# The MLP on unnormalised h: each token's squared norm factor moves behind w_down, and h is turned quarter by quarter

## The chip, the cores and the metric

The kernel runs on one core of one Trainium2 chip. The metric is the device time in microseconds (us) of one execution. The profile is one further execution, recorded by the hardware profiler.

## What is computed

A decoder block on 512 tokens of 1024 channels: two token mixers (a gated delta rule and a forgetting attention), merged by sigmoid gates, and behind them an MLP. All of it is float32. The change touches the last four lines alone:

```python
def rmsnorm(x, g):
    y = xf * lax.rsqrt(jnp.mean(xf * xf, axis=-1, keepdims=True) + EPS)
    return y * g
...
h = x + merged @ w_out[l]
hn = rmsnorm(h, norm_mlp_g[l])
x = h + jnp.square(jax.nn.relu(hn @ w_up[l])) @ w_down[l]
```

With r the factor rsqrt(mean(h²) + EPS) of a token, `hn` is r · (h · g). Since r is positive, relu(r · a)² = r² · relu(a)², so r² can be applied to a token's row behind `w_down`.

## The kernel before

**Arithmetic on TensorE.** Each float32 operand is split into a high and a low part (`hi` and `lo` of a weight, `shi` and `slo` of an activation), and a product is three matmuls: high by high, low by high, high by low. ScalarE (ACT) casts the high part (line 1165 for weights, 973 for activations), VectorE (DVE) subtracts to get the low part (1172 and 978).

**Seven products for eight.** From `w_o` (w_out) on, each big matrix product is done in the Strassen-Winograd way: a weight matrix is cut into quarters, and seven products P1 to P7 of sums of quarters stand for eight. Each of them is taken in two parts, s = 0 and s = 1. Weight sums are made by transfers: a plain load issued by SP, or one issued by POOL (GpSimd) that adds a further quarter to a tile in place, and can thus not start before the DVE has taken the low part of that tile's last contents. A part of a product needs one 128x1024 weight tile; its `hi` lies in one of four buffers, cast three parts ahead.

**Tokens and quarters.** The residual stream lies in `accs[tb][l]`: tb = 0 to 3 blocks of 128 tokens, l = 0, 1 halves of 512 channels. i = tb // 2 names a half of the tokens, and (i, l) a quarter of h. `w_o` and `w_d` (w_down) have the tokens on the partitions (`tokens_product`: 12 matmuls of 128x512 a part); after the second part of a product, its two PSUM tiles are added to one or two quarters of `accs` (`add_product`, `add_task`, DVE). `w_u` (w_up) has the features on the partitions (`blocks_product`: 24 matmuls of 128x256 a part) and reads h transposed: the tiles `hq[l][i, j]`. Those are made in `turn_h`: transposes on TensorE into PSUM tiles `hnT`, and ACT's copy to `hq` with the factor norm_mlp_g per partition (line 1112).

**PSUM.** All eight banks go in pairs: U for P1, then also for P6, P7 and P4, V for P5, then also for P3, W for P2, X for P4 of `w_o`. P3's first matmul goes on accumulating in V, so it waits for the additions that read P5 there; P7's waits likewise for P6's.

**Order.** `MLP` is the written list of parts: for `w_o` P1, P2, P1, P2 (parts 0, 0, 1, 1), then P5, P3, P6, P7, P4, two parts each; then `w_u` P1, P2, P5 and so on, `w_u` and `w_d` interleaved over four chunks of the hidden layer. The loop over it emits, for each part: what lies in `before` (the turns), the cast of the weight three ahead, the additions (`evicted`) of the part before, the low part, loads, up to three tasks out of `later`, and the matmuls. TensorE's order is kept as written (`PIN`); for DVE, ACT and POOL a scheduler sets the order at build time, and each engine then runs its queue in that order.

**The norm in the middle.** `h_done(i, l)` comes when a quarter of h has had its last addition: ACT squares and sums its rows (1085). When both quarters of a token half are done, `rms_h` makes r (DVE 1092 and 1093, then `rsq`, a power on POOL at line 306), `scale_h` writes r · h into pages `proj` (DVE, 1100, four of them), and `turn_h` turns the two quarters, 16 transposes of `proj` in one go.

Of the kernel before, what the change touches and what calls it, by code (L numbers as in the profile page):

```python
# [11 lines left out]
ALU = mybir.AluOpType  # L12
# [4 lines left out]
P = 128  # L17
T = 512
D = 1024
KT = D // P  # L20
H = 8
NCH = T // P
EPS = 1e-6
# [18 lines left out]
def hybrid_block(tc, a, out):  # L42
# [20 lines left out]
    def nm(s):  # L63
        n_names[0] += 1
        return f"{s}_{n_names[0]}"
# [5 lines left out]
    def page(dt=F32, s="pg"):  # L71
        if s in FOX_TAGS:
            return fxp.tile([P, T], dt, tag=s, name=nm(s))
        tag = TAGS_OF.get(s, s)
        if tag in TAGS:
            return pgp.tile([P, T], dt, tag=tag, name=nm(s), bufs=TAGS[tag])
        return pgp.tile([P, T], dt, tag="pg", name=nm(s))

    KEEP = ("ones", "expo", "ident", "c_norm_mlp_g", "rs_h", "ss_h")

    def const(shape, s, dt=F32):
        return (cp if s in KEEP else cm).tile(shape, dt, tag=s, name=s)

# [6 lines left out]
    def atps(s="at"):  # L90
        return pat.tile([P, T], F32, tag="at", name=nm(s))
# [7 lines left out]
    def cs(c):  # L99
        return slice(c * P, (c + 1) * P)  # L100
# [126 lines left out]
    def dense(nme, rhi, rlo, cols=P):  # L227
        hi, lo = unit(nme)
        ps = mmps()
        o = ps[:cols, :]  # L230
        for k in range(KT):
            w = hi[:, k * cols:(k + 1) * cols]
            mm(o, w, rhi(k), start=(k == 0), stop=False)  # L233
            mm(o, w, rlo(k), start=False, stop=False)  # L234
        tick()
        for k in range(KT):
            mm(o, lo[:, k * cols:(k + 1) * cols], rhi(k), start=False, stop=(k == KT - 1))  # L237
        return ps
# [14 lines left out]
    ones = const([P, P], "ones")  # L253
# [3 lines left out]
    expo = const([P, 16], "expo")  # L257
    vec.memset(expo, -0.5)
    ident = const([P, P], "ident")
# [45 lines left out]
    def rsq(dst, src):  # L305
        pool.tensor_tensor(dst, src, expo[:, 0:src.shape[-1]], op=ALU.pow)
# [40 lines left out]
    for pool_, tag, n in early:  # L347
        t = pool_.tile([P, n * T], F32R, tag=tag, name=nm("xs"))
# [12 lines left out]
    for k in range(KT):  # L361
        w = first[0][0][:, k * 64:(k + 1) * 64]
# [517 lines left out]
    def lst(ts_, j):  # L880
        return lambda k: ts_[k][j]
# [22 lines left out]
    for h in range(H):  # L904
        ps = dense("w_ga", uh, ul)
# [11 lines left out]
    for n in range(KT):  # L917
        ps = dense("w_pg", lst(oa, 0), lst(oa, 1))
# [10 lines left out]
    def accpage(s):  # L929
        return accp.tile([P, T], F32, tag="acc", name=nm(s))  # L930
# [5 lines left out]
    def of_half(pg_, f):  # L936
        return pg_[:, f * 256:(f + 1) * 256]
# [11 lines left out]
    pvec, pact, ppe = [Pinned(eng, pin) for eng, pin in zip((vec, act, nc.tensor), pins)]  # L949
    later = []  # L950
# [30 lines left out]
    def forms_later(qs, res, steps, parts=range(NSUB), front=False):  # L981
        new = [(form_task, qs[s_], res, p, s_, st) for p, st in steps for s_ in parts]
        later[:] = new + later if front else later + new
# [14 lines left out]
    for n in range(KT):  # L998
        ps = dense("w_gb", uh, ul)
# [4 lines left out]
    for n in range(KT):  # L1004
        s_, j, f = n // 4, n // 2 % 2, n % 2
        ps = dense("w_pf", lst(obs, 0), lst(obs, 1))
# [17 lines left out]
    accs = [[accpage("acc") for _ in range(2)] for _ in range(NCH)]  # L1024
# [6 lines left out]
    def apart(w, c):  # L1031

        return w == "w_o" or (w, c) == ("w_d", NC - 1)

    def banks(w, c, p, s_):
        b, first = ("X", True) if apart(w, c) and p == "P4" else BANKS[p]
        if first and s_ == 0:
            banks_of[w, c, b] = [atps("mlp"), atps("mlp")]
        return banks_of[w, c, b], first
# [11 lines left out]
                ppe.matmul(ps[t], slo[:, k], wh, start=False, stop=False, skip_group_check=True)  # L1051
                ppe.matmul(ps[t], shi[:, k], wl, start=False, stop=last, skip_group_check=True)

    def add_task(acc, ps, op):
        pvec.tensor_tensor(acc, acc, ps, op=op)  # L1055

    def count(w, c, i, l, done):
        n = left[w, c, i, l] = left.get((w, c, i, l), 0) + 1
# [3 lines left out]
    def add_product(w, c, p, ps, done):  # L1062

        add, sub = ALU.add, ALU.subtract
        for i, l, op in {"P1": [(0, 0, add)], "P2": [(0, 0, add)], "P5": [(1, 1, add)], "P3": [(0, 1, add)],
                         "P6": [(0, 1, sub)], "P7": [(1, 1, sub)] + ([(1, 0, add)] if apart(w, c) else []),
                         "P4": [(1, 0, add)]}[p]:
            for t in range(2):
                yield add_task, accs[2 * i + t][l], ps[t], op
            yield count, w, c, i, l, done  # L1070


    hq = quarters("hq")
    hforms = {}
    rs_h = const([P, NCH], "rs_h")
    ss_h = const([P, NCH, 2], "ss_h")

    before = []

    ready = [2, 2]  # L1080

    def h_done(i, l):
        for t in range(2):
            junk = page(s="junk")
            pact.activation(junk, accs[2 * i + t][l], AF.Square, accum_out=ss_h[:, 2 * i + t, l:l + 1])
        ready[i] -= 1
        if not ready[i]:
            later[:0] = [(rms_h, i), (scale_h, i, 0), (scale_h, i, 1)]

    def rms_h(i):  # L1090
        sl = slice(2 * i, 2 * i + 2)
        pvec.tensor_tensor(rs_h[:, sl], ss_h[:, sl, 0], ss_h[:, sl, 1], op=ALU.add)
        pvec.tensor_scalar(rs_h[:, sl], rs_h[:, sl], 1.0 / D, EPS, op0=ALU.mult, op1=ALU.add)
        rsq(rs_h[:, sl], rs_h[:, sl])

    def scale_h(i, l):
        hn = []
        for t in range(2):
            x = page(s="proj")
            pvec.tensor_scalar(x, accs[2 * i + t][l], rs_h[:, 2 * i + t:2 * i + t + 1], None, op0=ALU.mult)  # L1100
            hn.append(x)
        before.append((turn_h, i, l, hn))

    def turn_h(i, l, hn):
        for j in range(2):
            pt = atps("hnT")
            for f in range(2):
                for t in range(2):
                    ppe.transpose(pt[:, f * 256 + t * P:f * 256 + (t + 1) * P], hn[t][:, cs(2 * j + f)], ident)
            for f in range(2):  # L1110
                n = 4 * l + 2 * j + f
                pact.activation(of_half(hq[l][i, j], f), of_half(pt, f), AF.Copy, scale=mlp_g[:, n:n + 1])
        if l:
            forms_later(hq, hforms, SUMS if i else (("P1", "a"), ("P1", "b"), ("P2", "a"), ("P2", "b")), front=True)

    mlp = {}

# [35 lines left out]
    for k, (w, c, p, s_) in enumerate(MLP):  # L1153
# [26 lines left out]
        ps, first = banks(w, c, p, s_)  # L1180
        if w == "w_u":
            if p == "P1" and s_ == 0:
                mlp[c] = quarters("act"), {}
            qs, forms = mlp[c]
            blocks_product(c, p, s_, [hforms[k] for k in needs], ps, first)
            evicted = [(evict, p, qs[s_], ps[s_])]
            if s_ == NSUB - 1 and p in MADE:
                steps = MADE[p]
                if p == "P4" and c == NC - 1:
                    steps = sorted(steps, key=lambda st: ("P5", "P6", "P3", "P7", "P4").index(st[0]))  # L1190
                evicted.append((forms_later, qs, forms, steps))
        else:
            tokens_product(c, p, s_, res[p, s_], ps, first)
            done = h_done if w == "w_o" else give if c == NC - 1 else lambda i, l: None
            evicted = list(add_product(w, c, p, ps, done)) if s_ == NSUB - 1 else []
# [81 lines left out]
```

## Time and profile before

| | before |
|---|---|
| median of 3 runs | 1024.31 us (1021.71 to 1024.59) |
| profiled execution, and its span | 1024.1 us, 1022.4 us |
| mean granted clock of TensorE | 0.993 |
| TensorE busy | 1003.3 us, 98% of the span |
| DVE, ACT, POOL busy | 674.4, 561.5, 219.8 us |

The span runs from the first to the last instruction on the profile's own clock, and 1.7 us of the profiled execution lie around it. `w_o` begins at 651.7 us in the span, the first part of `w_u` at 694.3 us, and from there to the end TensorE has only products of the MLP. In lists of the trace a row gives the start and the length of an instruction (matmuls overlap, so their starts tell the pace), its line, its output and inputs, and in brackets how long its engine had idled before it and what ended that. The row of a timeline can hold several instructions (x16), whose length is then that of all. In a list of windows a row gives the length of the window, each engine's busy time in it and the granted clock (1.00 is full).

### The profile page before, as it was taken

How to read it: one execution, taken by the hardware profiler on the slowest of the kernel's cores; microseconds unless marked ns; L12 is line 12 of the kernel's file. 1: busy time of each engine (PE TensorE's matmuls, PEld its weight loads, DVE VectorE, ACT ScalarE, POOL GpSimd, SP SyncE). 2: the span in 40 equal slices, each digit the busy share in tenths (PEclk: the TensorE clock that was granted, in tenths of full speed). 3: DMA queues.
4: the chain of work that ended last, by engine and by line, in shares of the span. 5: the costliest groups of instructions: out<-in, count | busy, mean ns of one | idle time of the engine just before them, and what ended most of it. 6: DMA issues, size and time to landing. Idle time of an engine off the chain costs nothing.

```text
span 1022.4 us, 16241 instructions
## 1 busy us (share of the span) xinstructions
PE 1003.3 (98%) x6361; PEld 887.9 (87%) x6361; DVE 674.4 (66%) x1138; ACT 561.5 (55%) x855; POOL 219.8 (21%) x212
## 2 busy tenths in 40 slices
PE   8999999999999999999999999998999999999997
PEld 6788899998788999988888888778989989988985
DVE  6877677454657686354655225778897697687694
ACT  6765454546664455346753332557865665666751
POOL 1445130113532310113100004411121121121110
PEclk9999999999999999999999999999999999999999
DMA  6435322134433233123435534576888888788845
GB/s 214 144 110 150 96 81 84 56 108 128 124 101 114 58 111 95 53 93 114 126 113 172 196 103 157 120 180 123 195 177 206 181 175 216 171 176 197 191 89 127
DMA packets 58732, 138.67 MB, mean 136 GB/s; under 512 B 6208, under 2 KB 22816, under 8 KB 58656
## 3 DMA queue, kind: packets, MB, share of 16 engines
q1 hardware_dynamic: 48256, 99.88, 30.4%
q0 software_dynamic: 10400, 37.76, 20.8%
q8 instruction: 50, 0.82, 0.3%
q14 instruction: 26, 0.21, 0.1%
HBM read 129.18 MB, written 8.44 MB: 135 GB/s over the span
## 4 chain that ended last, share of the span: by engine, by line
PE 85%; DVE 4%; issue 4%; DMA 4%; POOL 1%; ACT 1%; SPq 0%; POOLq 0%; DVEq 0%; ACTq 0%
PE mlp L946 29%; PE mm L233 9%; PE mm L234 9%; PE mm L237 9%; PE fx L824 5%; PE fx L821 5%; PE fx L822 5%; DMA draw<-w_d 2%; PE fo L804 2%; PE sc L779 2%; DMA row<-rowd 1%; PE pT L795 1%; PE v L668 1%; DVE conv L521 1%; PE o L687 1%
## 5 line engine op out<-in xcount | busy, mean ns | idle before, releaser
L1165 ACT CAST hi<-draw 128x1024 fp32r<-128x1024 f32 x124 | 129.8, 1050 | 128.5 <-PE mlp L946 100.2
L1172 DVE TENSOR_TENSOR lo<-draw,hi 128x1024 fp32r<-128x1024 f32 x124 | 151.2, 1222 | 54.8 <-ACT hi L1165 54.7
L215 DVE TENSOR_TENSOR lo<-raw,hi 128x1024 fp32r<-128x1024 f32 (+1 forms) x90 | 111.8, 1247 | 88.8 <-PE mm L237 50.8
L214 ACT CAST hi<-raw 128x1024 fp32r<-128x1024 f32 (+1 forms) x90 | 91.8, 1029 | 112.9 <-PE mm L234 81.4
L233 PE MATMUL mm<-uhi,hi 128*128 128x512 f32 x344 | 136.0, 396 | 2.6 <-DVE conv L521 2.2
L234 PE MATMUL mm<-ulo,hi 128*128 128x512 f32 x344 | 136.5, 397 | 1.2 <-DVE ulo L248 1.2
L946 PE MATMUL mlp<-hi,shi 128*128 128x512 f32 x280 | 110.3, 394 | 4.2 <-DVE acc L1055 1.9
L946 PE MATMUL mlp<-lo,shi 128*128 128x512 f32 x280 | 109.7, 392 | 0.5 <-DVE lo L1172 0.5
L946 PE MATMUL mlp<-hi,slo 128*128 128x512 f32 x280 | 109.7, 392 | 0.0
L821 PE MATMUL fx<-hi,uhi 128*128 128x256 f32 x384 | 98.0, 290 | 0.3 <-DVE conv L521 0.3
L822 PE MATMUL fx<-hi,ulo 128*128 128x256 f32 x384 | 96.0, 285 | 0.0
L946 PE MATMUL mlp<-slo,hi 128*128 128x256 f32 x448 | 90.3, 283 | 0.0
L946 PE MATMUL mlp<-shi,lo 128*128 128x256 f32 x448 | 90.3, 283 | 0.0
L946 PE MATMUL mlp<-shi,hi 128*128 128x256 f32 x448 | 90.3, 283 | 0.0
L237 PE MATMUL mm<-uhi,lo 128*128 128x512 f32 x344 | 89.2, 395 | 0.0
L233 PEld LDWEIGHTS mm<-uhi,hi 128*128 128x128 f32 x344 | 64.7, 188 | 17.1 <-issue 3.8
L234 PEld LDWEIGHTS mm<-ulo,hi 128*128 128x128 f32 x344 | 64.7, 188 | 15.4 <-DVE ulo L248 2.1
L237 PEld LDWEIGHTS mm<-uhi,lo 128*128 128x128 f32 x344 | 63.7, 188 | 13.2 <-issue 0.5
L821 PEld LDWEIGHTS fx<-hi,uhi 128*128 128x128 f32 x384 | 73.5, 191 | 1.2 <-issue 0.9
L822 PEld LDWEIGHTS fx<-hi,ulo 128*128 128x128 f32 x384 | 73.5, 192 | 0.5 <-issue 0.2
L946 PEld LDWEIGHTS mlp<-shi,hi 128*128 128x128 f32 x448 | 70.6, 192 | 0.9
L946 PEld LDWEIGHTS mlp<-shi,lo 128*128 128x128 f32 x448 | 69.9, 192 | 0.0
(310 smaller groups left out, 2029.4 us busy)
## 6 DMA issues: line engine op xcount, KB each, us to landing
draw<-w_u POOLq DMA_DIRECT2D x32, 512.0 KB, 5.8
draw<-w_d POOLq DMA_DIRECT2D x32, 512.0 KB, 6.5
raw<-w_gdn SPq DMA_DIRECT2D x24, 512.0 KB, 3.6
raw<-w_fox SPq DMA_DIRECT2D x24, 512.0 KB, 3.6
draw<-w_u SPq DMA_DIRECT2D x24, 512.0 KB, 4.5
draw<-w_d SPq DMA_DIRECT2D x24, 512.0 KB, 4.3
row<-rowd SPq DMA_DIRECT2D x24, 256.0 KB, 5.1
raw<-w_ga SPq DMA_DIRECT2D x8, 512.0 KB, 3.7
```

The source lines that it names most:

```text
L214: act.copy(hi[:, c], raw[:, c])
L215: vec.tensor_tensor(lo[:, c], raw[:, c], hi[:, c].bitcast(F32), op=ALU.subtract)
L233: mm(o, w, rhi(k), start=(k == 0), stop=False)
L234: mm(o, w, rlo(k), start=False, stop=False)
L237: mm(o, lo[:, k * cols:(k + 1) * cols], rhi(k), start=False, stop=(k == KT - 1))
L779: mm(psc[:, :n], qT[:, s], kT[:, :n], start=True, stop=True)
L821: mm(o, uhi[k][:, cs(tb)], w, start=(k == 0), stop=False)
L822: mm(o, ulo[k][:, cs(tb)], w, start=False, stop=False)
L824: mm(o, uhi[k][:, cs(tb)], us[k // 4][1][:, (k % 4) * 256:(k % 4 + 1) * 256], start=False, stop=(k == KT - 1))
L946: return (lambda *args, **kw: tc.keep_in_program_order(f(*args, **kw))) if self.pinned[0] else f
L1165: pact.copy(hi, raws[m][0])
L1172: pvec.tensor_tensor(lo, raws[m][0], hi[:, :].bitcast(F32), op=ALU.subtract)
```

## The change

`h` goes into the MLP times norm_mlp_g alone. `rms_h`, `scale_h` and the pages `proj` are gone, POOL's power too. A quarter of h is turned as soon as its own additions are done: `h_done` only puts `turn_h` into `before`, so its 8 transposes stand on TensorE one part later, and they read `accs` itself. The squares are issued in `turn_h`. When all four quarters are turned, `factor_h` goes to the end of `later`: four small DVE operations on 128x4 values make r² = 1 / (mean + EPS) and −r², for additions and subtractions. Behind `w_d` each addition takes its product times that factor: a `scalar_tensor_tensor` in the place of a `tensor_tensor`, with the same two 128x512 operands and a per-partition scalar more. The additions behind `w_o` stay as they were.

```diff
-    def add_task(acc, ps, op):
-        pvec.tensor_tensor(acc, acc, ps, op=op)
+    def add_task(acc, ps, op, by=None):
+        if by is None:
+            pvec.tensor_tensor(acc, acc, ps, op=op)
+        else:
+            pvec.scalar_tensor_tensor(acc, ps, by, acc, op0=ALU.mult, op1=ALU.add)
...
-                yield add_task, accs[2 * i + t][l], ps[t], op
+                tb = 2 * i + t
+                by = () if w == "w_o" else (r2_h[:, 1 if op == sub else 0, tb:tb + 1],)
+                yield (add_task, accs[tb][l], ps[t], op) + by
...
     def h_done(i, l):
+        before.append((turn_h, i, l))
+
+    def squares_h(i, l):
         for t in range(2):
             junk = page(s="junk")
             pact.activation(junk, accs[2 * i + t][l], AF.Square, accum_out=ss_h[:, 2 * i + t, l:l + 1])
-        ready[i] -= 1
-        if not ready[i]:
-            later[:0] = [(rms_h, i), (scale_h, i, 0), (scale_h, i, 1)]
-
-    def rms_h(i):
-        sl = slice(2 * i, 2 * i + 2)
-        pvec.tensor_tensor(rs_h[:, sl], ss_h[:, sl, 0], ss_h[:, sl, 1], op=ALU.add)
-        pvec.tensor_scalar(rs_h[:, sl], rs_h[:, sl], 1.0 / D, EPS, op0=ALU.mult, op1=ALU.add)
-        rsq(rs_h[:, sl], rs_h[:, sl])
-
-    def scale_h(i, l):
-        hn = []
-        for t in range(2):
-            x = page(s="proj")
-            pvec.tensor_scalar(x, accs[2 * i + t][l], rs_h[:, 2 * i + t:2 * i + t + 1], None, op0=ALU.mult)
-            hn.append(x)
-        before.append((turn_h, i, l, hn))
-
-    def turn_h(i, l, hn):
+
+    def factor_h():
+        r, m = r2_h[:, 0, :], r2_h[:, 1, :]
+        pvec.tensor_tensor(r, ss_h[:, :, 0], ss_h[:, :, 1], op=ALU.add)
+        pvec.tensor_scalar(r, r, 1.0 / D, EPS, op0=ALU.mult, op1=ALU.add)
+        pvec.reciprocal(r, r)
+        pvec.tensor_scalar(m, r, -1.0, None, op0=ALU.mult)
+
+    def turn_h(i, l):
         for j in range(2):
             pt = atps("hnT")
             for f in range(2):
                 for t in range(2):
-                    ppe.transpose(pt[:, f * 256 + t * P:f * 256 + (t + 1) * P], hn[t][:, cs(2 * j + f)], ident)
+                    ppe.transpose(pt[:, f * 256 + t * P:f * 256 + (t + 1) * P], accs[2 * i + t][l][:, cs(2 * j + f)],
+                                  ident)
...
-        if l:
+        squares_h(i, l)
+        ready[i] -= 1
+        if not ready[i]:
             forms_later(hq, hforms, SUMS if i else (("P1", "a"), ("P1", "b"), ("P2", "a"), ("P2", "b")), front=True)
+        if not any(ready):
+            later.append((factor_h,))
```

On TensorE the turn of the second token half stood, before, as one block of 16 transposes behind both parts of P1 of `w_u` (`mlp_6879` is part 1). The rows are the last matmuls of that part and the first transposes:

```order
L946 MATMUL mlp_6879<-shi_6838,lo_6804 128x256 x2
L946 MATMUL hnT_6951<-ident,proj_6917 128x128
L946 MATMUL hnT_6951<-ident,proj_6919 128x128
L946 MATMUL hnT_6951<-ident,proj_6917 128x128
L946 MATMUL hnT_6951<-ident,proj_6919 128x128
L946 MATMUL hnT_6958<-ident,proj_6917 128x128
```

Now that half's last quarter, (1, 0), stands between the two parts of P1 (`mlp_6876` and `mlp_6877`), and the other three quarters stand further up: (0, 0) between the parts of P5 of `w_o`, (0, 1) between those of P7, (1, 1) between those of P4.

```order
L946 MATMUL mlp_6876<-shi_6782,lo_6777 128x256 x2
L946 MATMUL hnT_6910<-ident,acc_6456 128x128
L946 MATMUL hnT_6910<-ident,acc_6458 128x128
L946 MATMUL hnT_6910<-ident,acc_6456 128x128
L946 MATMUL hnT_6910<-ident,acc_6458 128x128
L946 MATMUL hnT_6917<-ident,acc_6456 128x128
L946 MATMUL hnT_6917<-ident,acc_6458 128x128
L946 MATMUL hnT_6917<-ident,acc_6456 128x128
L946 MATMUL hnT_6917<-ident,acc_6458 128x128
L946 MATMUL mlp_6877<-shi_6780,hi_6806 128x256 x2
```

So 8 transposes of `acc` stand one part earlier, and the block of 16 is gone.

On DVE the queue in the middle of `w_o`, before, from the additions of P1 (`mlp_6500`, `mlp_6501`) to the first of P5 (`mlp_6601`), with those of P2 (`mlp_6526`, `mlp_6527`) in between; `slo<-m` are the low parts of plain quarters of the merged activation:

```order
L1055 TENSOR_TENSOR acc_6452<-acc_6452,mlp_6500 128x512
L978 TENSOR_TENSOR slo_6623<-m_5878,shi_6599 128x512
L978 TENSOR_TENSOR slo_6625<-m_5882,shi_6621 128x512
L1055 TENSOR_TENSOR acc_6454<-acc_6454,mlp_6501 128x512
L978 TENSOR_TENSOR slo_6650<-m_5880,shi_6627 128x512
L978 TENSOR_TENSOR slo_6671<-m_5884,shi_6629 128x512
L1055 TENSOR_TENSOR acc_6452<-acc_6452,mlp_6526 128x512
L1172 TENSOR_TENSOR lo_6567<-draw_6405,hi_6566 128x1024
L1055 TENSOR_TENSOR acc_6454<-acc_6454,mlp_6527 128x512
L1172 TENSOR_TENSOR lo_6588<-draw_6488,hi_6587 128x1024
L1172 TENSOR_TENSOR lo_6616<-draw_6185,hi_6615 128x1024
L1055 TENSOR_TENSOR acc_6457<-acc_6457,mlp_6601 128x512
```

The same stretch now (P5's first tile is `mlp_6597`):

```order
L1056 TENSOR_TENSOR acc_6452<-acc_6452,mlp_6500 128x512
L1056 TENSOR_TENSOR acc_6454<-acc_6454,mlp_6501 128x512
L1177 TENSOR_TENSOR lo_6567<-draw_6405,hi_6566 128x1024
L1056 TENSOR_TENSOR acc_6452<-acc_6452,mlp_6526 128x512
L1056 TENSOR_TENSOR acc_6454<-acc_6454,mlp_6527 128x512
L1177 TENSOR_TENSOR lo_6588<-draw_6488,hi_6587 128x1024
L1177 TENSOR_TENSOR lo_6630<-draw_6185,hi_6629 128x1024
L978 TENSOR_TENSOR slo_6637<-m_5878,shi_6595 128x512
L1056 TENSOR_TENSOR acc_6457<-acc_6457,mlp_6597 128x512
```

The four additions of P1 and P2 moved ahead of the `slo<-m`, and three of the four `slo<-m` moved behind the first addition of P5.

On DVE around the second turn, before:

```order
L1172 TENSOR_TENSOR lo_6863<-draw_6734,hi_6862 128x1024
L1092 TENSOR_TENSOR rs_h<-ss_h 128x2
L1172 TENSOR_TENSOR lo_6913<-draw_6669,hi_6912 128x1024
L1093 TENSOR_SCALAR rs_h<-rs_h 128x2
L1172 TENSOR_TENSOR lo_6980<-draw_6692,hi_6979 128x1024
L1100 TENSOR_SCALAR proj_6917<-acc_6456,rs_h 128x512
L1100 TENSOR_SCALAR proj_6919<-acc_6458,rs_h 128x512
```

and now, from the additions of P4 on, for which the turn of (1, 0) waits:

```order
L1177 TENSOR_TENSOR lo_6847<-draw_6724,hi_6846 128x1024
L1056 TENSOR_TENSOR acc_6456<-acc_6456,mlp_6814 128x512
L1056 TENSOR_TENSOR acc_6458<-acc_6458,mlp_6815 128x512
L1177 TENSOR_TENSOR lo_6868<-draw_6744,hi_6867 128x1024
L1099 TENSOR_TENSOR r_h<-ss_h 128x4
L1100 TENSOR_SCALAR r_h<-r_h 128x4
L1101 RECIPROCAL r_h<-r_h 128x4
L1102 TENSOR_SCALAR r_h<-r_h 128x4
```

Between the last addition and the turn no DVE work is left; the factor's four operations stand behind it. Behind the first chunk's `w_u` all queues have the order of before, but for the new additions of `w_d`.

More of the change, by code (lines that the diff above doesn't have):

```diff
@@ L77, in page @@
         return pgp.tile([P, T], dt, tag="pg", name=nm(s))
-    KEEP = ("ones", "expo", "ident", "c_norm_mlp_g", "rs_h", "ss_h")
+    KEEP = ("ones", "ident", "c_norm_mlp_g", "ss_h", "r2_h")
     def const(shape, s, dt=F32):
@@ L1074, in hybrid_block @@
     hforms = {}
-    rs_h = const([P, NCH], "rs_h")
     ss_h = const([P, NCH, 2], "ss_h")
+    r2_h = const([P, 2, NCH], "r2_h")
     before = []
```

## The prediction

> **What bounds the kernel now.** I read the page first: which engine is full, and at what clock.
>
> ```profile
> PE 1003.3 (98%) x6361; PEld 887.9 (87%) x6361; DVE 674.4 (66%) x1138; ACT 561.5 (55%) x855; POOL 219.8 (21%) x212
> PEclk9999999999999999999999999999999999999999
> ```
>
> TensorE is busy for 98% of the span, and the change leaves its matmuls as they are: only its waits and its clock can move. So next the list of waits, TensorE's from 620 us on, and ACT's for a transfer:
>
> ```profile
> PE hnT L946 <- DVE proj L1100: 2.7, 1, 2.7
> PE mlp L946 <- DVE acc L1055: 1.9, 1, 1.9
> PE mlp L946 <- ACT hi L1165: 1.2, 1, 1.2
> PE mlp L946 <- DVE lo L1172: 0.5, 1, 0.5
> ACT hi L1165 <- DMA draw<-w_d: 14.6, 3, 8.2
> ```
>
> Two waits lie where the change works: the second turn's for `proj`, and P3's for the additions that read P5's bank. The other two are the end's. TensorE's timeline shows the places (a row's start is what counts; 0.23 us from one 512-wide matmul to the next is its full pace):
>
> ```profile
> 665.17 0.39 PE L946 MATMUL mlp<-lo,shi 128*128 128x512 f32 x1
> 665.40 0.39 PE L946 MATMUL mlp<-hi,shi 128*128 128x512 f32 x1
> ...
> 667.89 0.39 PE L946 MATMUL mlp<-lo,shi 128*128 128x512 f32 x1
> 670.23 0.47 PE L946 MATMUL mlp<-hi,shi 128*128 128x512 f32 x1 [1.95 <-DVE acc L1055]
> ...
> 687.06 1.91 PE L946 MATMUL hnT<-ident,proj 128*128 128x128 f32 x16
> 688.72 0.48 PE L946 MATMUL mlp<-hi,shi 128*128 128x512 f32 x1
> 689.04 0.39 PE L946 MATMUL mlp<-hi,slo 128*128 128x512 f32 x1
> ...
> 699.80 0.40 PE L946 MATMUL mlp<-shi,lo 128*128 128x256 f32 x2
> 702.87 3.46 PE L946 MATMUL hnT<-ident,proj 128*128 128x128 f32 x16 [2.67 <-DVE proj L1100]
> 706.09 0.48 PE L946 MATMUL mlp<-shi,hi 128*128 128x256 f32 x2
> ```
>
> The first 16 transposes take 1.66 us (687.06 to 688.72), the same 16 of the second turn 3.22 us. The windows say why: the granted clock (the third figure from the right) is half behind the wait, and full again at 706.
>
> ```profile
> 703.00:704.00 1.00, 1.00 (x5) 0.85 (x6) 0.92 (x3) 0.00 (x0) 0.60 (x1) 0.50 1.02 184
> ...
> 706.00:707.00 1.00, 1.00 (x12) 1.00 (x9) 0.97 (x2) 1.00 (x4) 0.00 (x0) 1.00 1.08 205
> 900.00:950.00 50.00, 50.00 (x299) 44.74 (x298) 41.25 (x50) 29.21 (x38) 11.25 (x13) 1.00 0.86 185
> ```
>
> The last row stands for the stream from 706 to 1003 us: TensorE full, DVE at 41.25 of 50. From the two waits above, TensorE is never held in it.
>
> **The change part by part.** *The second turn.* Its transposes waited through sum, power on POOL and scaling on DVE. Now the turn of (1, 0) needs only the two additions of P4, about 1.3 us of DVE by the rows below, and TensorE has a part of 24 matmuls between (12 x 0.24 = 2.88 us). The wait goes: last pair 699.80 plus its 0.24 is 700.04, so 702.87 − 700.04 = 2.83 us. Bounds: none of it, if the additions come 2.83 us too late; all of it, taken, since nothing else stands between on DVE. With the wait goes the half clock behind it: 3.22 − 1.66 = 1.56 us; ends 0 and 1.56, and I take 1.56, since the 16 transposes at 687.06, without a wait ahead, ran at full pace.
>
> The page "TensorE: Matmul & The Clock Gate" of the Trainium skill (Part 4, PE-mode transpose) says that transposes do not count as activity for the clock gate, so that the full rate does not engage for them; by that, all 32 transposes would run as the slow ones did, 6.4 us for my 3.3. The row at 687.06 speaks against it.
>
> *Four turns for two.* The transposes are the same 32. But the matmul behind a group starts its successor 0.32 us later (688.72 to 689.04) instead of 0.23: two groups more, 0.2 us; ends 0 and 0.4 us (double). The other three turns wait for additions a part earlier, 2.72 us (665.40 plus 12 x 0.227) against 1.3 us of DVE. The tightest is (0, 0), so I follow it in DVE's and ACT's rows of before:
>
> ```profile
> 661.20 0.68 DVE L1055 TENSOR_TENSOR acc<-acc,mlp 128x512 f32<-128x512 f32 x1
> 661.79 1.28 DVE L978 TENSOR_TENSOR slo<-m,shi 128x512 fp32r<-128x512 f32 x2
> 663.00 0.68 DVE L1055 TENSOR_TENSOR acc<-acc,mlp 128x512 f32<-128x512 f32 x1
> ...
> 665.40 1.22 DVE L1172 TENSOR_TENSOR lo<-draw,hi 128x1024 fp32r<-128x1024 f32 x1
> 666.53 0.68 DVE L1055 TENSOR_TENSOR acc<-acc,mlp 128x512 f32<-128x512 f32 x1
> 667.13 2.35 DVE L1172 TENSOR_TENSOR lo<-draw,hi 128x1024 fp32r<-128x1024 f32 x2
> 669.40 1.27 DVE L1055 TENSOR_TENSOR acc<-acc,mlp 128x512 f32<-128x512 f32 x2
> ...
> 662.71 1.05 ACT L1165 CAST hi<-draw 128x1024 fp32r<-128x1024 f32 x1 [0.86 <-PE mlp L946]
> 682.46 0.63 ACT L1085 ACTIVATE junk<-acc 128x512 f32<-128x512 f32 x1
> 683.60 0.19 ACT L1085 ACTIVATION_READ_ACCUMULATOR junk<-acc 128x1 f32 x1
> ```
>
> Start to start, an addition or a `slo` costs 0.6 us, a `lo` 1.13 us. The new queue from 661.20: two additions (662.4), `lo` (663.5), P2's two additions (664.75). The turn stands on TensorE at 665.40, where P5's first part ends: no wait, with 0.65 us in hand. In the old order the second of these additions ran 666.53 to 667.2, 1.8 us too late for it.
>
> *P3's wait for P5's bank.* On from 664.75: `lo` (665.9); the next `lo` needs a weight cast that follows two squares on ACT (about 664.25, 1.33 us for the two) and the end of P5's first part, 665.6, and takes 1.05 us: 666.65; `lo` 667.85, `slo` 668.45, P5's addition until 669.05. TensorE starts 0.14 us behind an addition (669.40 + 0.69 to 670.23): 669.2. It has meanwhile done the turn (8 transposes, 0.83 us) and P5's second part: 665.40 + 0.83 + 2.72 = 668.95. The wait is 0.25 us, where it was 670.23 − 668.12 = 2.11. So three `slo` moved behind and eight transposes in the gap are worth 1.86 us. Bounds: 0 (DVE as late as before, plus the turn) and 2.11; I take 1.86, as both queues are read to the end. Late next: P7 behind P6's additions, as before.
>
> *What goes on DVE and POOL, what comes.* Eight scalings and four small operations go, four small ones come, and two powers leave POOL. `factor_h` is first used by `w_d`, twelve parts of `w_u` at 2.88 us, some 35 us, later. This hides under the full TensorE; no cover is used up. The squares stay eight, on an ACT that is busy 15.78 of 20 us from 690 to 710 (row below). Weight transfers on POOL no longer stand behind the power; no cast between 706 and 980 us waited for a transfer, so that gives nothing.
>
> *The additions behind w_d.* 58 of the 74 become the three-operand form:
>
> ```profile
> L1055 DVE TENSOR_TENSOR acc<-acc,mlp 128x512 f32<-128x512 f32 x74 | 49.3, 680 | 6.1 <-PE mlp L946 5.8
> L899 DVE SCALAR_TENSOR_TENSOR z<-omT,c_gdn_norm_g,z 128x512 f32<-128x512 f32 x8 | 5.9, 743 | 3.0 <-PE omT L108 3.0
> L1100 DVE TENSOR_SCALAR proj<-acc,rs_h 128x512 f32<-128x512 f32 x8 | 3.3, 478 | 0.8 <-POOL rs_h L306 0.8
> ```
>
> L899 has the new form's operands (PSUM, a scalar per partition, SBUF): 743 ns for 680, so 58 x 0.063 = 3.7 us more on DVE. The row of 900 to 950 us leaves 8.75 of 50 us of DVE free, so it is hidden there. It counts where DVE leads at the end:
>
> ```profile
> 977.43 0.68 DVE L1055 TENSOR_TENSOR acc<-acc,mlp 128x512 f32<-128x512 f32 x1
> 979.83 0.68 DVE L1055 TENSOR_TENSOR acc<-acc,mlp 128x512 f32<-128x512 f32 x1
> ...
> 994.68 0.68 DVE L1055 TENSOR_TENSOR acc<-acc,mlp 128x512 f32<-128x512 f32 x1
> ...
> 1018.37 0.69 DVE L1055 TENSOR_TENSOR acc<-acc,mlp 128x512 f32<-128x512 f32 x1 [0.67 <-PE mlp L946]
> ...
> 1003.65 1.04 ACT L1165 CAST hi<-draw 128x1024 fp32r<-128x1024 f32 x1 [8.25 <-DMA draw<-w_d]
> ```
>
> The first three stand ahead of low parts that release the last accumulating transfers, for which the cast at 1003.65 waits; the fourth ends the kernel: 4 x 0.063 = 0.25 us. Bounds: 0.06 (the last alone) and 3.7 (all).
>
> Sum: −2.83 − 1.56 − 1.86 + 0.2 + 0.25 = −5.8 us on the profiled execution's 1024.1 us: 1018.3 us. The median of the runs shown is 1024.31, 0.2 above, so it stands for both. About 0.3%, 3 us, is what a measurement of this kernel can tell from no change: the three runs lie 1021.71 to 1024.59.
>
> **The rivals.** *P3 waits as before.* DVE stays late in `w_o`, 1.86 us are lost: 1020.2. For it: DVE has no pause from 661.20 to 669.40 in the rows above. Against: four additions and three `slo` changed places, and 1.8 us are moved out of the way.
>
> *DVE becomes the bound behind the turn.* TensorE comes 6 us earlier to P5 of `w_u`, whose sums, casts and low parts all follow the last turn. If DVE ends that block as late as before, less what the change takes from it (eight scalings, 3.3 us at L1100), the gain is 3.3 − 0.25 = 3.05: 1021.0. For it: DVE is 18.92 of 20 us busy from 710 to 730.
>
> ```profile
> 710.00:730.00 20.00, 20.00 (x169) 20.00 (x168) 18.92 (x25) 17.23 (x26) 3.46 (x4) 1.00 0.73 160
> 690.00:710.00 20.00, 17.33 (x117) 16.24 (x116) 15.58 (x25) 15.78 (x35) 3.45 (x4) 0.91 0.76 155
> ```
>
> Against: 690 to 710 has idle DVE time, and the turned quarters now come earlier.
>
> *The transfers set the end.* Then an earlier TensorE only waits longer at 1003 us: 1024.3. For it: the 8.25 us. Against: those transfers are released by low parts that follow TensorE's own pace, and no earlier cast waits for one.
>
> *The transposes do not get the full clock* (the page's rule as a mechanism of this kernel): each 16 take 3.22 us, both turns, so 1018.3 + 2 x 1.56 = 1021.4.
>
> *Slower: the turns wait.* If the additions of a quarter come as late as `proj` did, TensorE, which runs its queue in order, stands 2.83 us at that turn and goes on at half clock, 1.56 us: 4.39 us. At all four turns that is 17.6 us: 1018.3 + 17.6 = 1035.9. Two such turns (8.8 us, 1027.1) are enough to be measurably slower than before. It decides where an addition ends later than 2.72 + 2.83 us behind its product. For it: the second of these additions ran at 666.53, 1.8 us late for the new turn; if all four kept to that, without the half clock (P3's wait of 2.11 us had none behind it), 7.2 us would give 1025.5, about no change. Against: the new queues put the additions first.
>
> **How the numbers follow.** Forecast 0.52; P3's wait stays 0.14; DVE bound 0.14; transfers 0.07; transposes slow 0.05; turns late 0.08, 0.02 of it the mild form. Faster by over 0.3% is below 1021.2: 0.52 + 0.14 and 0.10 of the DVE case, 0.76; slower 0.06; the rest 0.18. Predicted is the forecast, 1018.3. The range goes up to 1022, which leaves out transfers and late turns (0.15), and takes in the bounds of P3's wait and the clock. Down it goes to 1015.5: the runs shown reach 2.6 us below their median.
>
> **What would show it.** Right: `hnT` as four groups of 8 reading `acc`, each about 0.83 us long, no wait of TensorE over 0.5 us between 660 and 1000 us, granted clock 1.00 through 690 to 710, P2 of `w_u` at about 700 instead of 706.09, additions behind `w_d` at 743 ns, the wait at the end as before. Wrong: a wait of `hnT` for `acc` with a slow stretch behind it, a new wait of `mlp` for `slo` in `w_u`, or a longer wait of the last casts.

## The result, and the profile after

| | before | after |
|---|---|---|
| median (lowest to highest), first comparison | 1023.87 us (1021.71 to 1024.59), 6 runs | 1016.06 us (1014.29 to 1020.86), 6 runs |
| ratio, 95% interval | | 0.9934 (0.9919 to 0.9949) |
| profiled execution, and its span | 1024.1, 1022.4 us | 1015.88, 1014.2 us |
| mean granted clock of it | 0.993 | 0.998 |

The change makes the kernel 7.8 us faster by the medians (5.2 to 8.3 us by the interval), where 5.8 were forecast. On the page, TensorE keeps its 98% and loses 4.8 us of busy time, though it has the same matmuls; that is a matter of the clock: 0.993 before, 0.998 after.

```profile
PE 998.5 (98%) x6361; PEld 884.0 (87%) x6361; DVE 675.1 (67%) x1130; ACT 560.8 (55%) x855; POOL 219.1 (22%) x210
```

TensorE's waits from 620 us on, which is the view that named the two places before:

```profile
PE mlp L946 <- ACT hi L1170: 1.6, 1, 1.6
PE mlp L946 <- DVE sgb L1008: 0.9, 1, 0.9
PE mlp L946 <- DVE lo L1177: 0.5, 1, 0.5
```

The wait of `hnT` for `proj` and that of P3 for `acc` are gone. What is left is the end's (`hi`, `lo`) and one ahead of `w_o` (`sgb`), which before has too. TensorE's timeline at the turn of (0, 0), at P3 and at the turn of (1, 0):

```profile
662.90 0.40 PE L946 MATMUL mlp<-lo,shi 128*128 128x512 f32 x1
663.14 1.03 PE L946 MATMUL hnT<-ident,acc 128*128 128x128 f32 x8
663.93 0.48 PE L946 MATMUL mlp<-hi,shi 128*128 128x512 f32 x1
...
666.54 0.39 PE L946 MATMUL mlp<-lo,shi 128*128 128x512 f32 x1
666.86 0.47 PE L946 MATMUL mlp<-hi,shi 128*128 128x512 f32 x1
...
693.55 0.40 PE L946 MATMUL mlp<-shi,lo 128*128 128x256 f32 x2
693.79 1.04 PE L946 MATMUL hnT<-ident,acc 128*128 128x128 f32 x8
694.58 0.48 PE L946 MATMUL mlp<-shi,hi 128*128 128x256 f32 x2
...
697.54 0.40 PE L946 MATMUL mlp<-shi,hi 128*128 128x256 f32 x2
```

The turns start at the pace of the matmuls ahead of them. P3 starts 0.32 us behind P5's last matmul, where 0.23 is full pace: it waited 0.09 us. P2 of `w_u` starts at 697.54, before at 706.09. The window of that stretch has the full clock and a full TensorE, and the group of the new additions has the length of the row that stood for them:

```profile
690.00:710.00 20.00, 20.00 (x165) 19.83 (x164) 18.63 (x29) 16.50 (x30) 4.38 (x5) 1.00 0.79 160
L1058 DVE SCALAR_TENSOR_TENSOR acc<-mlp,r_h,acc x58: 740/746/751, 738.8 to 1010.1; 128x512 f32<-128x512 f32 x58
```

To see where time went in all kernels, I cut each span at three rows of TensorE's timeline: the first matmul of `w_o`, the first of `w_u`, and the 25th pair of `w_u` (a row `x2`), with which P2 begins (before 706.09, after 697.54). All in us, to 0.1:

| kernel (its section is below) | to `w_o` | `w_o` | `w_u` to P2 | the rest |
|---|---|---|---|---|
| before | 651.7 | 42.6 | 11.8 | 316.3 |
| before, repeated | 652.1 | 42.6 | 11.9 | 316.2 |
| after | 649.5 | 41.5 | 6.6 | 316.7 |
| after, repeated | 650.0 | 41.5 | 6.6 | 316.5 |
| turned in halves, two profiles | 652.1, 650.8 | 44.2, 42.6 | 7.5, 7.5 | 318.2, 320.5 |
| two tasks a part | 650.3 | 50.7 | 7.4 | 317.2 |
| the additions alone | 651.0 | 42.6 | 12.0 | 317.7 |
| same layout | 652.7 | 41.5 | 6.6 | 315.3 |
| short, long wait | 650.5, 653.8 | 41.5, 41.5 | 7.4, 11.1 | 318.1, 315.6 |
| P4 first | 652.3 | 41.5 | 6.6 | 313.0 |

From before to after the second and third columns lose 1.1 and 5.2 us, 6.3 together, and the last grows by 0.4. The first column, in which the code is the same, lost 2.2 us as well: that had to be explained.

### The profile page after: what moved, and what is told of

Its sections match the earlier page's. It is cut to its first block, busy times and chain, and to the rows that moved or that the text cites. A ratio compares the mean times of both kernels' runs of the same rounds, so it can differ in the third digit from the quotient of the medians.

```text
span 1014.2 us, 16230 instructions
## 1 busy us (share of the span) xinstructions
PE 998.5 (98%) x6361; PEld 884.0 (87%) x6361; DVE 675.1 (67%) x1130; ACT 560.8 (55%) x855; POOL 219.1 (22%) x210
## 4 chain that ended last, share of the span: by engine, by line
PE 86%; issue 4%; DMA 4%; DVE 4%; POOL 1%; ACT 1%; SPq 0%; POOLq 0%; DVEq 0%; ACTq 0%
PE mlp L946 29%; PE mm L233 10%; PE mm L234 9%; PE mm L237 9%; PE fx L821 5%; PE fx L824 5%; PE fx L822 5%; DMA draw<-w_d 2%; PE fo L804 2%; PE sc L779 2%; DMA row<-rowd 1%; PE pT L795 1%; PE v L668 1%; DVE conv L521 1%; PE o L687 1%
```

## The experiments

### Before and after once more

The kernel before, with no edit.

> The kernel before once more, for the granted clock of each of its runs. Theory: some 2 us of the 7.8 us between the medians are no part of the change but half-clock stretches in the unchanged first 650 us, which come in some executions and not in others; then the runs of this kernel spread over some 3 us in step with their clock, and in a profile of it w_o begins between 649 and 652 us. Rival: the first 650 us are always slower than in the changed kernel; then w_o begins at 651.7 us again, within 0.3 us, and the clock does not follow the time.

Measured: 1023.44 us (10 runs) against 1024.09 (35 runs), ratio 0.9995 (0.9984 to 1.0005). The two waits and the columns from `w_o` on came out as in the first profile. `w_o` began at 652.1 us, just past the theory's 649 to 652 and 0.4 us from the rival's 651.7, so this profile alone decides nothing. But the times lie 4.7 us apart (1020.66 to 1025.40) and go roughly with their clock: 0.998 in the shortest run, 0.991 to 0.993 in the four above 1024. And the kernel after, with no edit:

> The changed kernel unchanged, for a second profile and more times. Its first profile came 2.3 us earlier to w_o than that of before, in code that is the same in both, and its total gain (7.8 us) is some 1.8 us larger than the gain in the stretch from w_o to P2 of w_u (6.3 us). Theory (the surplus is chance: half-clock stretches that fall or don't fall in the unchanged part): w_o begins at 650 to 652.5 us this time, the stretch from w_o to P2 of w_u takes 48.1 us again, and the median over all runs comes to 1016.5 to 1018, ratio 0.993 to 0.9945. Rival (the change made the first 650 us faster, by its other memory layout or loads): w_o begins at 649.5 again, and the median stays at 1016.

Measured: 1016.68 us (1015.68 to 1017.48, 6 runs) against 1023.22 (17 runs), ratio 0.9928 (0.9912 to 0.9944). `w_o` begins at 650.0, at the edge of what the theory allowed and 0.5 us from the rival's 649.5; the ratio lies just under the theory's range, and the two middle columns are the same to 0.1 us. More profiles decide it. The first column lies between 650.3 and 652.1 us in the six profiles with the old turns or the turns in halves, and between 649.5 and 653.8 in the six with the turns by quarters: it has nothing to do with the change. What makes it vary shows in windows of 5 us, first of before, then of after, at the same place:

```profile
405.00:410.00 5.00, 5.00 (x107) 4.50 (x107) 0.83 (x2) 1.17 (x2) 0.00 (x0) 0.89 0.22 56
410.00:415.00 5.00, 5.00 (x38) 4.42 (x37) 1.68 (x7) 1.54 (x4) 0.00 (x0) 0.77 0.00 0
```

```profile
405.00:410.00 5.00, 5.00 (x111) 4.51 (x110) 1.53 (x5) 1.58 (x4) 0.00 (x0) 1.00 0.17 48
410.00:415.00 5.00, 5.00 (x45) 4.31 (x44) 2.80 (x8) 1.55 (x4) 0.00 (x0) 1.00 0.01 3
```

TensorE is full in all four, but before ran part of it at half clock (0.89 and 0.77), and had another such stretch between 9 and 13 us, among short waits. Windows of 1 us give the number of these stretches ahead of `w_o` in all twelve profiles. With none of them `w_o` begins at 649.5 and 650.0 us (the two of after), with one at 650.3 to 651.0, with two at 651.7 to 652.7, with three at 653.8: about 1.3 us each. The kernels with turns by quarters have none, one, two and three of them. They come and go in unchanged code, so 2 us of the first profile's gain are chance.

### One part alone: turned in halves

The arithmetic of after, but both quarters of a token half turned together, 16 transposes in one go, when the second is done:

```diff
 def h_done(i, l):
-    before.append((turn_h, i, l))
+    ready[i] -= 1
+    if not ready[i]:
+        before.extend([(turn_h, i, 0), (turn_h, i, 1)])
...
```

> The changed arithmetic, but both quarters of a token half are turned together, 16 transposes in one go: behind the first part of P7 of w_o, and behind the first part of P1 of w_u. Theory (three separate terms): the second turn's wait and its half clock are gone (-4.4 us), P3's wait for P5's bank is back at about 2.1 us, since the queue of VectorE around it reads as before: 1016.06 + 1.9 - 0.2 = 1017.8 us. Rival: turning quarter by quarter is worth nothing by itself: 1016.1 us, no wait of P3. Second rival: the wait and the clock come from 16 transposes in a row: 1020.5 us, half clock at the second turn.

Measured: 1022.76 us (1019.65 to 1025.69, 12 runs) against 1024.09, ratio 0.9991 (0.9978 to 1.0003): most of the gain is gone, which the theory had not foreseen. TensorE's timeline at P3 of `w_o`, then at P3 of `w_u`:

```profile
668.30 0.39 PE L946 MATMUL mlp<-lo,shi 128*128 128x512 f32 x1
670.62 0.47 PE L946 MATMUL mlp<-hi,shi 128*128 128x512 f32 x1 [1.93 <-DVE acc L1056]
...
671.99 0.63 PE L946 MATMUL mlp<-hi,slo 128*128 128x512 f32 x1
...
716.86 0.50 PE L946 MATMUL mlp<-shi,hi 128*128 128x256 f32 x2 [1.39 <-ACT act L1129]
```

Both turns run without a wait (the column to P2 has 7.5 us instead of 11.8: the 4.3 us forecast for the second turn are there). But P3 waits again, and DVE's rows say why. First this kernel, then after:

```profile
662.19 1.28 DVE L978 TENSOR_TENSOR slo<-m,shi 128x512 fp32r<-128x512 f32 x2
663.40 0.68 DVE L1056 TENSOR_TENSOR acc<-acc,mlp 128x512 f32<-128x512 f32 x1
663.99 1.28 DVE L978 TENSOR_TENSOR slo<-m,shi 128x512 fp32r<-128x512 f32 x2
665.20 0.68 DVE L1056 TENSOR_TENSOR acc<-acc,mlp 128x512 f32<-128x512 f32 x1
665.80 1.21 DVE L1178 TENSOR_TENSOR lo<-draw,hi 128x1024 fp32r<-128x1024 f32 x1
666.93 0.68 DVE L1056 TENSOR_TENSOR acc<-acc,mlp 128x512 f32<-128x512 f32 x1
667.53 2.35 DVE L1178 TENSOR_TENSOR lo<-draw,hi 128x1024 fp32r<-128x1024 f32 x2
669.80 1.27 DVE L1056 TENSOR_TENSOR acc<-acc,mlp 128x512 f32<-128x512 f32 x2
```

```profile
661.26 1.28 DVE L1056 TENSOR_TENSOR acc<-acc,mlp 128x512 f32<-128x512 f32 x2
662.46 1.22 DVE L1177 TENSOR_TENSOR lo<-draw,hi 128x1024 fp32r<-128x1024 f32 x1
664.29 1.22 DVE L1177 TENSOR_TENSOR lo<-draw,hi 128x1024 fp32r<-128x1024 f32 x1 [0.61 <-ACT hi L1170]
665.43 0.69 DVE L978 TENSOR_TENSOR slo<-m,shi 128x512 fp32r<-128x512 f32 x1
666.03 0.68 DVE L1056 TENSOR_TENSOR acc<-acc,mlp 128x512 f32<-128x512 f32 x1
```

With no early turn behind them, the additions of P1 and P2 stand between the `slo<-m` again, as before, and P5's addition comes at 669.80. In after they stand ahead of them, and P5's comes at 666.03: its end at 666.71 plus the 0.14 us of the prediction is P3's 666.86, within 0.01. So the gain at P3 is the early turn's, through DVE's queue.

The second loss is new: 1.39 us at 716.86. In `w_u` too P3 goes on in P5's bank, and there it is ACT that takes P5 out of it (`act`, line 1129). By ACT's rows that copy came 1.95 us behind the end of P5's first part in after, and 3.8 us here. In ACT's queue it now stands behind two casts of sums (`shi<-s`) and a second weight cast, which waits for TensorE. That it stands there because DVE can make those sums only when both quarters are turned is likely, but no run shows it. The rest is the clock: 671.99 is one of eight matmuls at half pace, 1.6 us in the column of `w_o`. Whether that belongs to the kernel, a second profile was to say:

> The run with two turns of 16 transposes once more, for a second profile. In its first profile P3 waited 1.93 us and 3.3 us at half clock followed, 1.6 us, where before and its repetition had waits of 1.9 us there without a slow stretch behind. If the slow stretch belongs to this kernel, the stretch from w_o to the start of w_u takes 44.2 us again; if it was chance, 42.6 us, as in before.

It was chance: 42.6 us for `w_o`, P3's wait of 1.95 us with no slow stretch behind it. This one execution took 1023.14 us, as its end was longer (a wait of 3.0 us for the last casts, then half clock for 6.8 us). Two profiles don't tell what the end costs on average here. The column and the wait, −4.3 + 1.4 = −2.9 us, would give 1021.2; the median is 1.6 us above that and the interval reaches down to 1021.8 only, so a part of the loss stays unplaced.

### Another way to free P3: two tasks a part

The kernel before, with up to two tasks out of `later` a part of `w_o` instead of three, so that fewer `slo<-m` stand ahead of the additions:

```diff
-  while any(k not in res for k in needs) or later and used + cost(later[0]) <= (3 if w == "w_o" else 3 if w == "w_u" and c == 0 else PER_UNIT):
+  while any(k not in res for k in needs) or later and used + cost(later[0]) <= (2 if w == "w_o" else 3 if w == "w_u" and c == 0 else PER_UNIT):
```

> The kernel before, with at most two tasks a part in w_o for three: low parts move behind the additions in VectorE's queue, nothing else of the change is done. Theory: P3's wait is a matter of that queue alone, and falls from 2.1 us to under 0.6 us: 1.5 to 2 us faster than before, about 1022.1 us, the second turn's wait of 2.7 us as before. Rival: the wait fell because 8 transposes stood in it: no change, 1023.9 us.

Measured: 1027.40 us (12 runs), ratio 1.0035 (1.0019 to 1.0051), slower. TensorE's rows at P3, the first turn and behind it:

```profile
667.13 0.47 PE L946 MATMUL mlp<-hi,shi 128*128 128x512 f32 x1 [0.20 <-DVE acc L1055]
...
683.31 2.25 PE L946 MATMUL hnT<-ident,proj 128*128 128x128 f32 x16 [1.16 <-DVE proj L1100]
691.01 0.79 PE L946 MATMUL mlp<-hi,slo 128*128 128x512 f32 x1 [5.22 <-DVE slo L978]
```

P3's wait fell to 0.20 us with the old arithmetic and the old turns: once more it is DVE's order that makes it. But the low parts that were put off are needed, and 5.2 us are waited for the last of them, with half clock behind (50.7 us for `w_o`). That the forecast left out, and it made the kernel slower. The second turn's wait, forecast to stay, is gone, as TensorE comes 8 us later to that turn. After puts off only three of the `slo<-m`, and only to behind P5's first addition.

### Does the wait bring the half clock? A short and a long wait

After, with the quarter (1, 0) sent through POOL ahead of its turn: first as two plain copies per tile, which I took for dearer than they are:

```diff
...
+    if (i, l) == (1, 0):
+        for t in range(2):
+            x = page(s="proj")
+            pool.tensor_copy(x, src[t])
+            pool.tensor_copy(x, x)
+            src[t] = x
...
```

> The changed kernel, with the quarter (1, 0) copied twice by GpSimd ahead of its turn (four copies of some 1.25 us), so that TensorE waits at that turn for about 3 us. Theory: a wait of some 2.7 us or more brings half clock for 3.3 us behind it: +3 us of wait and +1.6 us of clock, 1020.7 us, granted clock 0.50 behind the turn. Rival: the half clock at the old second turn had nothing to do with the wait: +3 us, 1019 us, clock 1.00. VectorE and the transfers behind GpSimd have their slack, so nothing else should show.

Measured: 1016.98 us (1016.55 to 1019.16, 4 runs), ratio 0.9925 (0.9906 to 0.9944). Three of the four copies took 0.61 us, one 1.61; the turn's transposes came only 0.8 us late (7.4 for 6.6 us to P2), the clock stayed full there, and the run does not decide the question. So the same with two-operand operations, which are exact here (h + h, then minus h):

```diff
-            pool.tensor_copy(x, src[t])
-            pool.tensor_copy(x, x)
+            pool.tensor_tensor(x, src[t], src[t], op=ALU.add)
+            pool.tensor_tensor(x, x, src[t], op=ALU.subtract)
```

> The changed kernel, in which the quarter (1, 0) goes through two POOL operations of two operands per tile (h + h, then minus h) ahead of its turn. In the run with plain copies the first began 0.33 us behind the start of w_u; four operations at 1.25 us (row of POOL's two-operand form in the trace of before) end 5.3 us behind it, while TensorE is through with its part at 2.87: a wait of about 2.5 us, the size of the 2.67 us wait of before. Theory (half clock follows such a wait, as at 702.87 us in before): the 8 transposes take about twice 0.83 us and the matmuls behind them go at half pace for some 2 us more, so from the start of w_u to P2's first part it takes 6.62 + 2.5 + 1.6 = 10.7 us, and the median is some 4 us above that of the changed kernel, about 1021. Rival (the half clock of before at this place had nothing to do with the wait): the clock stays at 1.00 behind the wait, 9.1 us for that stretch, a median of about 1019.5.

Measured: 1022.38 us (1019.68 to 1024.41, 10 runs) against 1023.22, ratio 0.9989 (0.9975 to 1.0004). TensorE's rows, and the windows of 1 us behind the wait:

```profile
697.91 0.40 PE L946 MATMUL mlp<-shi,lo 128*128 128x256 f32 x2
699.92 0.33 PE L946 MATMUL hnT<-ident,proj 128*128 128x128 f32 x1 [1.61 <-POOL proj L1110]
701.14 1.23 PE L946 MATMUL hnT<-ident,proj 128*128 128x128 f32 x7 [0.89 <-POOL proj L1110]
702.02 0.78 PE L946 MATMUL mlp<-shi,hi 128*128 128x256 f32 x2
...
704.30 0.63 PE L946 MATMUL mlp<-shi,lo 128*128 128x256 f32 x2
```

```profile
701.00:702.00 1.00, 0.86 (x7) 0.86 (x8) 1.00 (x2) 0.28 (x1) 0.09 (x1) 0.87 0.28 115
702.00:703.00 1.00, 1.00 (x6) 1.00 (x5) 0.24 (x1) 1.00 (x4) 0.46 (x1) 0.50 0.00 0
...
705.00:706.00 1.00, 1.00 (x10) 1.00 (x10) 1.00 (x3) 0.00 (x0) 0.00 (x0) 0.92 0.99 193
```

2.5 us of idle time in two pieces, with one transpose between them, then half clock for 3.4 us: the column to P2 is 11.1 us for the 10.7 expected and the 9.1 of the rival. By the rows' starts, as the prediction counted its 2.83, the wait is 2.9 us (1.77 ahead of the first transpose, 1.12 behind it), so of the 4.5 us that the column grew 1.6 are the clock's. The median is 5.7 us above that of after in the same comparison (1016.68); 1.2 of them are not placed. One wait gives back most of the gain of the change. This run builds in the slower rival's mechanism, and it confirms the two terms −2.83 and −1.56 from the other side.

### The additions alone, and the memory layout

The kernel before, with the three-operand additions behind `w_d` and a factor of plus or minus 1:

```diff
...
-  yield add_task, accs[2 * i + t][l], ps[t], op
+  by = () if w == "w_o" else (pm[:, 1:2] if op == sub else pm[:, 0:1],)
+  yield (add_task, accs[2 * i + t][l], ps[t], op) + by
...
```

> The kernel before, with the three-operand additions behind w_down and a constant factor of 1 or -1; the norm stays where it was. Theory: 743 ns for 680 ns each, hidden but at the end, +0.1 to +0.3 us: 1024.1 us, which cannot be told from no change. Rival: VectorE is near its bound in the stream, and up to 58 x 0.063 = 3.7 us show: 1027.6 us, with waits of TensorE for low parts between 706 and 1003 us.

Measured: 1025.03 us (12 runs), ratio 1.0012 (1.0000 to 1.0025). The 58 additions took 744 ns each, no new wait came in the stream, and at the end TensorE's row reads:

```profile
1006.10 0.59 PE L946 MATMUL mlp<-hi,shi 128*128 128x512 f32 x1 [2.89 <-ACT hi L1172]
```

where before has 1.23 us. The last column has 317.7 us for 316.3. That is more than the forecast 0.25; but the last cast waited 2.9 to 3.1 us in three of the nine profiles with these additions and 1.3 to 1.6 us in five of them (the ninth is P4 first, below), so a single profile says little. The three profiles with the old additions have 1.1 to 1.3 us there, too few to rule out that the new ones bring the long wait. The interval, 0 to 2.6 us, holds 0.25 and not the rival's 3.7.

After drops a constant from its tables, which moves what lies behind it in memory. With that constant kept:

```diff
-  KEEP = ("ones", "ident", "c_norm_mlp_g", "ss_h", "r2_h")
+  KEEP = ("ones", "expo", "ident", "c_norm_mlp_g", "ss_h", "r2_h")
```

> The changed kernel, with the constant column expo back in the pool in which it lay before. That is the only thing by which the change reaches into the first 650 us: without it 779 of 1293 shared tiles lie at other addresses than before, with it 5. Theory: addresses do not matter, and the 2.3 us by which w_o began earlier in the changed kernel's profile are half-clock stretches that come and go: 1016 us again, within 1 us. Rival: the layout was worth them: 1018.3 us, and w_o begins at 651.7 us.

Measured: 1017.27 us (1016.07 to 1018.60, 6 runs) against 1024.66, ratio 0.9930 (0.9915 to 0.9944). The ratio is that of after repeated (0.9928). `w_o` began at 652.7 us, which was the rival's sign, and the median is 1.2 us above 1016.06; but two stretches of half clock lie ahead of `w_o` in this profile, and from `w_o` to P2 it has the 41.5 and 6.6 us of after. No part of the layout in the gain is seen; one of under 1.5 us the interval would not show.

### What is left: the end

In the last chunk of `w_d`, P7 stands ahead of P4, and the last accumulating transfers are waited for. With P4 ahead of P7 there:

```diff
+  MLP[-4:] = MLP[-2:] + MLP[-4:-2]
```

> The changed kernel, with P4 ahead of P7 in the last chunk of w_down. In both profiles TensorE waits near the end (1.6 and 0.5 us) and then goes at half clock (about 1.7 us) for P7's weight, whose transfer is issued behind P4's two and lands last. Theory: P4's weights are there in time, and P7's land 5.4 us before they are needed: both waits and the half clock go (-3.8 us), the four additions of P7 stand last instead of two (+0.8 us): 1013 us. Rival: the transfers bound the end and the wait only moves to P4 or P7: 1016.1 us.

Measured: 1013.65 us (1011.94 to 1015.25, 5 runs) against 1024.66, ratio 0.9891 (0.9874 to 0.9908), the fastest of all. TensorE's whole list of waits from 620 us on is one row, and the last casts wait less for their transfers (ACT's timeline):

```profile
PE mlp L947 <- DVE sgb L1009: 0.9, 1, 0.9
```

```profile
999.10 1.05 ACT L1171 CAST hi<-draw 128x1024 fp32r<-128x1024 f32 x1 [2.86 <-DMA draw<-w_d]
1001.58 1.05 ACT L1171 CAST hi<-draw 128x1024 fp32r<-128x1024 f32 x1 [1.43 <-DMA draw<-w_d]
```

The last column is 313.0 us for 316.7, 3.7 us less for 3.0 forecast: both waits of the end (2.1 us) and the half clock behind them are gone.

## Why the prediction was right

Step by step, by its own terms:

- *The second turn's wait*, −2.83, and *the half clock behind it*, −1.56: from the first pair of `w_u` to P2 it took 11.8 us, now 6.6. Of these 5.2 us, 0.8 are eight transposes that moved into `w_o` (group to group 0.79 us), and 4.4 are left for the two terms, 4.39 forecast. The wait put back by POOL, 2.9 us by the rows' starts, took 4.5.
- *P3's wait*, −1.86 (2.11 to 0.25): it came to 0.09, so −2.0. The walk through DVE's queue had P5's addition end 3.65 us behind the turn's start (669.05 and 665.40), the trace has 3.57 (666.71 and 663.14). `w_o` lost 1.1 us although it took over the eight transposes.
- *Four turns for two*, +0.2: nothing to be seen. Four groups at 0.79 and two at 1.66 us, each with 0.09 us behind it, are 3.5 us either way. This was the one term that was not there: the prediction counted the matmul behind a group for the new groups, but not that eight transposes take less than half of sixteen.
- *Additions at the end*, +0.25: 744 to 746 ns each for the 743 of the row; the last column has 0.2 to 0.5 us more in the two profiles of after. That the end's waits differ as much from profile to profile (1.2, 1.1; 1.6, 1.3 us) leaves the size of this term open.
- *Squares, factor, POOL at nothing*: the four operations of `factor_h` stand in 0.8 us of DVE time from 693.2 to 694.0, and no row of TensorE waits there.

The sum in the two middle columns is −6.3 us for −6.05 forecast (the sum without the 0.25 of the end). The total of the first profile, 8.2 us, is larger by the stretches at half clock in the unchanged part; the medians give 7.8, in the repetition 6.5 and with the layout of before 7.4 us. So 0.2 to 1.5 us of them have no place in the columns; chance stretches are large enough for that. The mechanism was right, and that the first median lay 2 us beyond the forecast is no part of it.

The rivals: P3 did not wait as before. DVE is busier behind the turn (18.63 of 20 us from 690 to 710) and not the bound. The transfers kept their distance to TensorE: the cast at the end waited 8.22 us for one, as before 8.25, but TensorE behind it only 1.6. The 32 transposes ran at 270 to 273 ns each with the clock at 1.00. The Trainium skill ("TensorE: Matmul & The Clock Gate", Part 4) says that the full rate does not engage for transposes, as they don't count as activity for the clock gate. The first half is not borne out: 8 or 16 of them in a row, with matmuls around them, ran at full pace. Whether they count as activity these runs don't test: 16 of them last 1.66 us, and waits of 1.95 us had no half clock behind them in four profiles of five either. And no turn waited for its additions: in DVE's queue they moved ahead where a turn by quarters stands behind them, and stayed behind with the turns in halves.

## What to carry to other kernels

When an engine is full but for a few waits, ask of each wait whether a slow clock follows it: a wait of 2.9 us, by the rows' starts, cost 4.5 here. A consumer that is written earlier also pulls its producers forward where a scheduler orders the queues, and what that displaces can free a buffer that a third party waits for; so follow the queue beyond the operation that you move. And set a gain in one execution against the stretches of the profile in which the code is the same: here 2 us of 8 were not the change's.

## What was not expected of the hardware

Half clock comes in stretches of 3.4 us (two were of 6.8), and what brings them is not only the length of a wait. Behind every single wait of 2.67 us and more in the twelve profiles (2.67 at the turn in three, 2.9 to 3.1 at the end in three, 5.2 in one) the clock was half, and so it was behind the 1.61 and 0.89 us with one transpose between. Behind P3's wait of about 1.95 us it was in one profile of five, behind a wait of 2.03 us at 9.74 us in after repeated it was not; behind the 1.1 to 1.6 us at the end, with mostly 0.5 us more soon after, it was in six profiles of eight. The page "TensorE: Matmul & The Clock Gate" of the Trainium skill (Part 1, on oscillation) asks for no idle gaps above about 3.4 us; the runs here show that 2.67 us are too long already.

Ahead of `w_o`, half clock with TensorE full came at two places alone, near 190 us (in five profiles of twelve) and near 410 us (in eight). Each time it began within 0.8 us of the end of a run of 96 matmuls of 32x32, which takes 3.0 us; there are two such runs. Here is the second in before, where the clock is half from 408.9 us on:

```profile
405.99 2.01 PE L628 MATMUL Tp<-XT,Q 32*32 32x32 f32 x61
...
407.94 1.08 PE L632 MATMUL Tq<-Q,XT 32*32 32x32 f32 x29
408.94 1.65 PE L779 MATMUL sc<-fk,fq 128*128 128x384 f32 x2
```

In after the same run, from 405.21 us, has full clock behind it, and the last row takes 0.91 us there. The two runs of 64 such matmuls (2.1 us) had no half clock behind them in any profile. So a row of small matmuls can be followed by half clock although the profile calls TensorE full. No run here changes these matmuls, so it is not shown that they bring it, and why it follows them in 13 cases of 24 stays open.
